# Scoring both differential heads of a pair in one run of 24 row-tiled products, in four banks, in a two-layer hybrid encoder

## The chip, the cores and the metric

The kernel runs on one core of one Trainium2 chip. The metric is the device time of one execution in microseconds (us). Engines are named as in the profile: PE is TensorE, DVE VectorE, ACT ScalarE, POOL GpSimd, SP SyncE, which issues most DMAs.

## The reference

Two layers are applied to x of 256 tokens by 2048 columns, in float32. Each layer projects the normed x to 7168 columns, feeds three groups of heads, and projects their joined outputs back. The group that the change touches is the differential attention: six heads, each with two halves of 64 columns in q and k, and one v of 128 columns.

```python
q = rmsnorm(d_q.reshape(b, s, DIFF_HEADS, 2, DIFF_HALF_DIM), diff_q_norm_g[l])
k = rmsnorm(d_k.reshape(b, s, DIFF_HEADS, 2, DIFF_HALF_DIM), diff_k_norm_g[l])
sc = jnp.einsum('bhcqd,bhckd->bhcqk', qi, kt) * scale + bias[None, :, None]
p = jax.nn.softmax(sc, axis=-1)
o = jnp.einsum('bhcqk,bhkd->bhcqd', p, vt)
return o[:, :, 0] - lam * o[:, :, 1]
...
y_d = rmsnorm(o_d, diff_head_norm_g[l]) * (1.0 - lam_init) * silu(d_g)
x = x + jnp.concatenate([y_a, y_d, y_m], axis=-1) @ w_out[l]
```

`bias` is minus the head's slope times the distance of the two positions. The other groups are a short gated convolution and a cross-attention of four heads into 256 memory tokens.

## The kernel before

**The stream of products.** Nearly all the time goes into products of float32 matrices. Each operand is split into hi and lo parts, and three products (hi·hi, hi·lo, lo·hi) stand for one (`products`, L301 to L307). Weights come in pieces of 256 rows by 512 columns: `load_w` (L286) has SP load a piece into `raw`, ACT round it to `hi` (L294) and DVE subtract to `lo` (L295). `raw` has four buffers, and so have `hi` and `lo` (`PARTS // CK`). `block` (L309) walks over the pieces of one block of 512 columns; a piece gives 12 products of 128x512 on PE. In this document these are the ordinary products, and "a piece" is 12 of them. The layer's input projection has 112 pieces, its output projection 27 more and some products of another form. Before the first layer, the memory tokens' keys and values are projected in the same way.

**Side work.** Everything else is written as generators that are stepped between the pieces. `later(g, n)` makes a generator due n pieces from now; `run_side` (L231) is called once per piece and steps those that are due; a `yield n` asks to be called n pieces later. Within the program, a scheduler that works from a time line may still shift instructions that are not pinned against each other; `pin` keeps an instruction in the written order of the pinned ones of its engine.

**The differential heads.** The projections of q and k are normed, turned to columns by DVE transposes of 32x32 blocks and a trip through DRAM (`turn_sheet`, `carry`), and split into `yT` (`qk_T`, L530). Then three generators `pair` per layer (L558) do two heads each. They begin at the fifth block of the projection (L1069 to L1074), nine pieces apart (`PAIR_EVERY`, L39); the two memory pairs follow in the same rhythm. A pair does this:

- For each head, wait for a free buffer `e` (there are two), then `diff_scores` (L599): 12 products of 64 rows (L606), two halves c of the head in the upper and lower 64 rows of PE's array, two blocks of tokens, three products each, into two banks of PSUM from the pool `ps_s` (tag s). Then DVE adds the bias out of PSUM (L611), takes the maximum (L613), ACT takes the exponentials with their sums (L617), and DVE forms the difference of the two halves (L620 to L624). Between the heads the generator lets two pieces pass.
- Turn both heads' weights (`sh`, L573) and carry them through DRAM (L498, L502).
- `weighted` (L514): four products of the weights with v into one bank of the pool `ps_t` (tag t) for each head, `po` (L519; the profile counts eight), and `diff_out` (L628), which norms and gates them; the result is turned and split into `yT` again.

**PSUM.** There are eight banks: four for the ordinary products, two in `ps_s`, two in `ps_t`. `ps_s` also serves the memory heads' scores (L661 to L663), `ps_t` also `po` of both kinds of heads.

Of the kernel before, what the change touches and what calls it, by code (L numbers as in the profile page):

```python
# [10 lines left out]
F32 = mybir.dt.float32  # L11
# [7 lines left out]
P = 128  # L19
D_MODEL = 2048  # L20
SEQ = 256
DEPTH = 2
NT = SEQ // P
# [4 lines left out]
CG = W_CONV // P  # L28
# [10 lines left out]
PAIR_EVERY = 9  # L39
# [9 lines left out]
def encoder(ctx: ExitStack, tc: tile.TileContext, x, mem, norm_g, w_in, conv_w, conv_b,  # L49
            dq_g, dk_g, lq1, lk1, lq2, lk2, head_g, mem_norm_g, w_mem_kv, mq_g, mk_g, w_out, out):  # L50
    nc = tc.nc
    x, mem, out = x[0], mem[0], out[0]

    def pool(name, bufs, space=None):
        kw = {"space": space} if space is not None else {}
        return ctx.enter_context(tc.tile_pool(name=name, bufs=bufs, **kw))
# [9 lines left out]
    ps_s = pool("ps_s", 2, PSUM)  # L66
    ps_t = pool("ps_t", 2, PSUM)
# [3 lines left out]
    def nm(s):  # L71
        uid[0] += 1
        return f"{s}_{uid[0]}"
# [136 lines left out]
    side, tasks = deque(), []  # L210
    due = {}
    chunk = [0]

    def later(g, n):
        due[id(g)] = chunk[0] + n
        return g
# [30 lines left out]
    made = set()  # L247
# [50 lines left out]
    def accumulators():  # L298
        return [ps_acc.tile([P, NB], F32, tag="acc", name=nm("acc")) for _ in range(NT)]
# [127 lines left out]
    def col(st, which, t):  # L427
        return st[:, which, t:t + 1]
# [64 lines left out]
    def carry(sheet, to):  # L493


        d = dram.tile([NA, B, NA, sheet.shape[-1]], F32, name=nm("d"))
        for a in range(NA):
            tc.keep_in_program_order(nc.sync.dma_start(d[:, :, a].rearrange("b c r -> c b r"), sheet[a * B:(a + 1) * B]))  # L498
        yield 2
        of = d.rearrange("b c a (n i) -> (b c) a n i", i=B)  # L500
        for a in range(NA):
            tc.keep_in_program_order(nc.sync.dma_start(to[:, :, a], of[:, a]))  # L502
# [25 lines left out]
    ROWS = (slice(0, HALF), slice(HALF, P))  # L528
# [25 lines left out]
    scored = set()  # L554

    held = {"e": 0, "sh": 0, "yn": 0}

    def pair(heads, begin, end, v):  # L558

        es = []  # L560
        for h in heads:
            while held["e"] == 2:
                yield 1
            held["e"] += 1
            es.append((yield from begin(h)))
            yield 2
        yield 4
        while held["sh"] == 2:
            yield 1
        held["sh"] += 1  # L570
        sh = tmp.tile([P, NA, 2, NT * NT, B], F32, tag="sh", name=nm("sh"))
        for i, e in enumerate(es):
            tc.keep_in_program_order(nc.vector.transpose(  # L573
                sh[:, :, i], e[0].rearrange("p t (k b c) -> p b (t k) c", k=NT, b=NA)))
            held["e"] -= 1
            yield 1
        yield 4
        flat = sh.rearrange("p b h n c -> p (b h n c)")
        yield from carry(sh.rearrange("p b h n c -> p b (h n c)"), flat.rearrange("p (n a i) -> p n a i", a=NA, i=B))
        eT = flat.rearrange("p (h t k q) -> p h t k q", h=2, t=NT, k=NT)  # L580
        while held["yn"] == 2:
            yield 1
        held["yn"] += 1
        yn = tmp.tile([P, NA, 2, NT, B], F32, tag="yn", name=nm("yn"))
        for i, h in enumerate(heads):
            end[0](h, yn[:, :, i], weighted(eT, i, v, h), *es[i][1:])
            yield 2
        held["sh"] -= 1
        yield 5
        tc.keep_in_program_order(nc.vector.transpose(yn, yn))  # L590
        yield 5
        flat = yn.rearrange("p b h t c -> p (b h t c)")
        yield from carry(yn.rearrange("p b h t c -> p b (h t c)"), flat.rearrange("p (n a i) -> p n a i", a=NA, i=B))
        for i, h in enumerate(heads):
            end[1](h, flat[:, i * SEQ:(i + 1) * SEQ])
            yield 1
        held["yn"] -= 1

    def diff_scores(l, h, yT):  # L599
        while not {("q", l, h), ("k", l, h)} <= made:  # L600
            yield 1
        s = [ps_s.tile([P, NT, SEQ], F32, tag="s", name=nm("s")) for _ in range(2)]
        for i in range(NT):
            for n, (a, b) in enumerate(((0, 0), (0, 1), (1, 0))):
                for c, rows in enumerate(ROWS):
                    pin(nc.tensor.matmul(s[c][:, i, :], yT[rows, a, h, i * P:(i + 1) * P], yT[rows, b, CG + h, :],  # L606
                                         start=n == 0, stop=n == 2))
        scored.add((l, h))
        e = tmp.tile([P, 2, NT, SEQ], F32, tag="e", name=nm("e"))
        for c in range(2):  # L610
            nc.vector.scalar_tensor_tensor(e[:, c], dist, -slopes[h], s[c], ALU.mult, ALU.add)  # L611
        mx = small.tile([P, 2, NT], F32, tag="mx", name=nm("mx"))
        nc.vector.tensor_reduce(mx, e, AX.X, ALU.max, negate=True)  # L613
        sm = small.tile([P, 2, NT], F32, tag="sm", name=nm("sm"))
        for c in range(2):
            for i in range(NT):
                nc.scalar.activation(e[:, c, i], e[:, c, i], AF.Exp, bias=mx[:, c, i:i + 1],  # L617
                                     accum_out=sm[:, c, i:i + 1])
        iv = small.tile([P, 2, NT], F32, tag="iv", name=nm("iv"), bufs=6)
        nc.vector.reciprocal(iv, sm)  # L620
        cf = small.tile([P, NT], F32, tag="cf", name=nm("cf"))
        nc.vector.scalar_tensor_tensor(cf, sm[:, 0], neglam[:, l:l + 1], iv[:, 1], ALU.mult, ALU.mult)
        for i in range(NT):
            nc.vector.scalar_tensor_tensor(e[:, 0, i], e[:, 1, i], cf[:, i:i + 1], e[:, 0, i], ALU.mult, ALU.add)  # L624
        return e[:, 0], iv
        yield

    def diff_out(h, yn, po, iv, st, a):  # L628
        ss = small.tile([P, NT], F32, tag="hss", name=nm("hss"))
# [180 lines left out]
    pin = tc.keep_in_program_order  # L810
# [48 lines left out]
    class Memory:  # L859
# [47 lines left out]
        def begin(self, half, part, w):  # L907

            if part == 0 and w == 0:
                self.acc[0, half] = accumulators()  # L910
            w_part = self.parts[0][w][:, half]
            for t in range(NT):
                pin(nc.tensor.matmul(self.acc[0, half][t], memT[:, part, 0, t * P:(t + 1) * P], w_part,  # L913
                                     start=part == 0 and w == 0, stop=False))
# [101 lines left out]
    s = 1  # L1016
    while s < DEPTH * KT:
        l, k = divmod(s, KT)
# [22 lines left out]
        s = group[-1] + 1  # L1041

    for l in range(DEPTH):
# [5 lines left out]
        yT = T_tile("yT")  # L1049
# [3 lines left out]
            return block(xT, w_in[l], cols, order, rows=x_row_tiles, **how)  # L1053

        def begin_pair(n, p):
            tasks.append(later(p, max(1, start + PAIR_EVERY * n - chunk[0])))


        order = range(6) if l == 0 else (3, 0, 1, 2, 4, 5)
# [1 line left out]
        for b in order:  # L1061
            if b in begun:
                acc = x_block([(C_D + b * NB, NB)], ALLK[-QT:], acc=begun[b])
            else:
                acc = x_block([(C_D + b * NB, NB)], ready=m.ready if l == 0 and b == order[0] else None)
            if b == 3:
                v = keep.tile([P, NT, W_DIFF], F32, tag="v", name=nm("v"))
                ga = keep.tile([P, NT, W_DIFF], F32, tag="ga", name=nm("ga"))
            if b == 4:  # L1069
                start = chunk[0]  # L1070
                for n in range(DH // 2):
                    begin_pair(n, pair((2 * n, 2 * n + 1), lambda h: diff_scores(l, h, yT),
                                       (lambda h, yn, po, iv: diff_out(h, yn, po, iv, st, ga),
                                        lambda h, y: split_T(yT, CG + h, y, hgain[:, l:l + 1], pin=True)), v))  # L1074
            if b < 3:
                tasks.append(later(qk_T(l, yT, normed(acc, HALF, st, sheets(("mqT", "mga", "e")[b])),
                                 (0, 0, 4) if b == 0 else (0, 4, 2) if b == 1 else None,
                                 (256, 0, 2) if b == 1 else (0, 2, 4) if b == 2 else None), 8))
            else:
                for t in range(NT):  # L1080
                    if b == 3:
                        nc.scalar.activation(v[:, t, 0:NB], acc[t], AF.Copy, scale=col(st, R, t))
                    elif b == 4:
                        nc.scalar.activation(v[:, t, NB:768], acc[t][:, 0:256], AF.Copy, scale=col(st, R, t))
                        silu2(ga[:, t, 0:256], acc[t][:, 256:512], st, t)
                    else:
                        silu2(ga[:, t, 256:768], acc[t], st, t)
# [12 lines left out]
        for t in range(NT):  # L1100
            a = tmp.tile([P, NB], F32, tag="nat", name=nm("a"), bufs=3)
# [97 lines left out]
        heads, convs = list(range(CG, KT)), list(range(CG))  # L1199
# [33 lines left out]
        x = [pl.tile([P, NB], F32, tag=tag, name=nm("x")) for pl, tag in ((ps_s, "s"), (ps_s, "s"), (ps_t, "t"), (ps_t, "t"))]  # L1233
# [71 lines left out]
```

## Time and profile before

| what | value |
|---|---|
| median of 3 runs | 923.93 us (923.77 to 924.42) |
| the profiled execution | 924.17 us, of which span 922.4 us |
| mean granted clock of PE | 0.999 |
| ordinary products of w_in and w_out, L305, memory part included | 3717 |
| scores of 64 rows, L606 | 144, first and last start at 210.1 and 685.1 us |
| DVE, share of the span | 77% |
| ACT, share of the span | 54% |

The span runs from the first to the last instruction. The profiled execution is the one that the trace shows; its time of 924.17 us stands beside the span of 922.4, and the 1.8 us between them lie around the instructions. A row of PE's timeline merges equal instructions that follow each other: the second number is then the time from the first one's start to the last one's end. Ordinary products overlap: each is shown as 0.39 us long, but the next one starts before it ends. What a thing costs on PE is therefore read from starts, not from durations.

### The profile page before, as it was taken

The page shows a single profiled execution, that of the slowest core. Times are in us where ns is not written, and L with a number is a line of the kernel's source. Part 1 is how long each engine was busy: PE and PEld are TensorE (multiplying, and loading weights), DVE is VectorE, ACT ScalarE, POOL GpSimd, SP SyncE. Part 2 cuts the span into 40 slices and gives each one's busy share as a digit, 9 for nine tenths or more (in the row PEclk, how much of TensorE's full clock was granted, in tenths as well). Part 3 has the DMA queues.
Part 4 walks back from the last instruction along what each step waited for, and adds up shares of the span by engine and source line. Part 5 has one row for each costly group of instructions (what it writes and reads, how often), then busy time and mean ns, then how long its engine had stood idle before and what let it go on. Part 6 is the DMA issues. An engine that isn't in the chain of part 4 may idle for free.

```text
span 922.4 us, 12464 instructions
## 1 busy us (share of the span) xinstructions
PE 917.2 (99%) x4209; PEld 755.4 (82%) x4209; DVE 713.4 (77%) x1281; ACT 494.0 (54%) x770; POOL 38.2 (4%) x68
## 2 busy tenths in 40 slices
PE   9999999999999999999999999999999999999998
PEld 6888888887788888888888888888788888888887
DVE  5579978757799797577789857778898788588686
ACT  5667644545545555545556544446545655446352
POOL 2434010000000000000000000000000000000000
PEclk9999999999999999999999999999999999999999
DMA  8989878885679999969777867986769898968842
GB/s 288 288 241 268 273 238 237 252 238 162 183 204 244 245 258 275 245 212 253 245 222 229 274 196 217 267 234 194 194 203 255 221 264 250 272 217 250 273 160 92
DMA packets 244560, 215.16 MB, mean 233 GB/s; under 512 B 131976, under 2 KB 171720, under 8 KB 244496
## 3 DMA queue, kind: packets, MB, share of 16 engines
q1 hardware_dynamic: 239520, 208.71, 78.7%
q0 software_dynamic: 3776, 4.59, 2.1%
q10 hardware_dynamic: 1200, 1.07, 0.3%
q8 instruction: 33, 0.54, 0.3%
q14 instruction: 31, 0.25, 0.1%
HBM read 193.30 MB, written 21.00 MB: 232 GB/s over the span
## 4 chain that ended last, share of the span: by engine, by line
PE 99%; ACT 0%; DVE 0%; issue 0%
PE acc L305 92%; PE x L351 1%; PE s L606 1%; PE po L519 1%; PE acc L351 1%; PE po L729 1%; PE acc L913 1%; PE pt L743 0%; PE s L663 0%; PE s L661 0%; PE s L662 0%; PE warm L128 0%; PE rest L305 0%; ACT hi L895 0%; DVE xs L1211 0%; ACT memT L261 0%
## 5 line engine op out<-in xcount | busy, mean ns | idle before, releaser
L305 PE MATMUL acc<-hi,xT 128*128 128x512 f32 x1792 | 561.6, 391 | 0.0
L294 ACT CAST hi<-raw 128x1024 fp32r<-128x1024 f32 x270 | 283.8, 1051 | 310.2 <-PE acc L305 244.8
L295 DVE TENSOR_TENSOR lo<-raw,hi 128x1024 fp32r<-128x1024 f32 x270 | 329.1, 1221 | 136.7 <-ACT hi L294 134.9
L305 PEld LDWEIGHTS acc<-hi,xT 128*128 128x128 f32 x1792 | 336.0, 188 | 71.2
L305 PE MATMUL acc<-lo,xT 128*128 128x512 f32 x896 | 349.1, 390 | 0.0
L305 PEld LDWEIGHTS acc<-lo,xT 128*128 128x128 f32 x896 | 168.3, 188 | 33.5
L305 PE MATMUL acc<-hi,yT 128*128 128x512 f32 (+1 forms) x432 | 134.2, 388 | 0.0
L305 PEld LDWEIGHTS acc<-hi,yT 128*128 128x128 f32 x432 | 81.0, 188 | 16.6
L305 PE MATMUL acc<-lo,yT 128*128 128x512 f32 x216 | 83.7, 388 | 0.0
L305 PE MATMUL acc<-hi,memT 128*128 128x512 f32 x248 | 78.1, 393 | 0.0
L305 PEld LDWEIGHTS acc<-hi,memT 128*128 128x128 f32 x248 | 46.1, 188 | 9.4
L896 DVE SCALAR_TENSOR_TENSOR lo<-raw,cva,hi 128x1024 fp32r<-128x1024 f32 (+1 forms) x34 | 41.0, 1219 | 15.2 <-ACT hi L895 15.1
L305 PE MATMUL acc<-lo,memT 128*128 128x512 f32 x124 | 48.0, 391 | 0.0
L305 PEld LDWEIGHTS acc<-lo,yT 128*128 128x128 f32 x216 | 40.6, 188 | 8.4
L895 ACT ACTIVATE hi<-raw,cva 128x1024 fp32r<-128x1024 f32 (+1 forms) x34 | 36.4, 1099 | 11.7 <-DMA raw<-in_w_mem_kv_dram 11.4
L305 PEld LDWEIGHTS acc<-lo,memT 128*128 128x128 f32 x124 | 23.3, 188 | 5.6 <-DVE lo L896 0.9
L377 ACT CAST hi<-wide 128x1024 fp32r<-128x1024 f32 x15 | 15.6, 1050 | 16.9 <-DVE wide L380 7.0
L617 ACT ACTIVATE e<-e,mx 128x256 f32<-128x256 f32 x48 | 23.8, 498 | 0.9 <-DVE mx L613 0.9
L760 POOL DMA_DIRECT2D xt<-in_x_dram x32 | 21.4, 676 | 19.7 <-DVE rsy L189 13.3
L377 DVE TENSOR_TENSOR lo<-wide,hi 128x1024 fp32r<-128x1024 f32 x15 | 18.1, 1221 | 3.9 <-ACT hi L377 3.7
L481 DVE STREAM_TRANSPOSE sh<-sh 128x1024 f32<-128x1024 f32 (+2 forms) x14 | 17.3, 1238 | 0.0
L264 ACT ACTIVATE xT<-xf,gx 128x256 fp32r<-128x256 f32 x32 | 14.3, 502 | 5.4 <-DVE xf L766 4.3
(202 smaller groups left out, 715.6 us busy)
## 6 DMA issues: line engine op xcount, KB each, us to landing
raw<-in_w_in_dram SPq DMA_DIRECT2D x192, 512.0 KB, 4.7
raw<-in_w_out_dram SPq DMA_DIRECT2D x54, 512.0 KB, 4.8
raw<-in_w_in_dram SPq DMA_DIRECT2D x64, 256.0 KB, 3.8
raw<-in_w_mem_kv_dram SPq DMA_DIRECT2D x30, 512.0 KB, 6.2
d<-sh SPq DMA_DIRECT2D x88, 128.0 KB, 4.1
sh<-d SPq DMA_DIRECT2D x72, 128.0 KB, 4.1
wide<-in_w_out_dram SPq DMA_DIRECT2D x10, 512.0 KB, 6.2
xs<-in_x_dram SPq DMA_DIRECT2D x4, 512.0 KB, 6.9
```

The source lines that it names most:

```text
L264: both = (nc.scalar.activation(hi, src, AF.Copy, scale=gain), nc.vector.scalar_tensor_tensor(lo, src, gain, hi.bitcast(F32), ALU.mult, ALU ...
L294: nc.scalar.copy(hi, raw)
L295: nc.vector.tensor_tensor(lo_, raw, hi.bitcast(F32), ALU.subtract)
L305: i = nc.tensor.matmul(acc, left, right, start=start, stop=stop)
L351: nc.tensor.matmul(acc, left[a], right[b], start=first and i == 0, stop=last and i == 2)
L377: return ((hi, pin(nc.scalar.copy(hi, src))), (lo, pin(nc.vector.tensor_tensor(lo, src, hi.bitcast(F32), ALU.subtract))))
L481: tc.keep_in_program_order(nc.vector.transpose(src, src))
L519: nc.tensor.matmul(po[:, t, :], eT[:, i, t, k, :], v[:, k, h * P:(h + 1) * P], start=k == 0, stop=k == NT - 1)
L617: nc.scalar.activation(e[:, c, i], e[:, c, i], AF.Exp, bias=mx[:, c, i:i + 1], accum_out=sm[:, c, i:i + 1])
L760: tc.keep_in_program_order(nc.gpsimd.dma_start(st[:, n], src[n * B:(n + 1) * B].rearrange("p (b r) -> b p r", b=NA)))
L895: both = (nc.scalar.activation(hi[:, j], raw[:, j], AF.Copy, scale=g), nc.vector.scalar_tensor_tensor(lo[:, j], raw[:, j], g, hi[:, j].bit ...
L896: nc.vector.scalar_tensor_tensor(lo[:, j], raw[:, j], g, hi[:, j].bitcast(F32), ALU.mult, ALU.subtract))
```

## The change

Both heads of a pair are scored before either is weighted. The pair first waits until no buffer `e` is in use, and takes both. `diff_scores` then issues 24 products without a break in the written order, for the second head first, into two banks of `ps_t`, then for the first head, into the two banks of `ps_s`. The rest of the former function is now `diff_weights`, run for one head after the other with two pieces between. The number that spaces the pairs grows by 2/3 for the third one, `round(9 * 2.667)` = 24 pieces behind the first instead of 18. The memory pairs begin where they did, 27 and 36 pieces behind the first.

```diff
@@ def pair(heads, begin, end, v):
-        for h in heads:
-            while held["e"] == 2:
-                yield 1
-            held["e"] += 1
-            es.append((yield from begin(h)))
+        while held["e"] > 0:
+            yield 1
+        held["e"] += len(heads)
+        scores = yield from begin[0](heads)
+        for h, s in zip(heads, scores):
+            es.append(begin[1](h, s))
             yield 2
         yield 4
@@
-    def diff_scores(l, h, yT):
-        while not {("q", l, h), ("k", l, h)} <= made:
+    def diff_scores(l, heads, yT):
+        while not {(x, l, h) for x in "qk" for h in heads} <= made:
             yield 1
-        s = [ps_s.tile([P, NT, SEQ], F32, tag="s", name=nm("s")) for _ in range(2)]
-        for i in range(NT):
-            for n, (a, b) in enumerate(((0, 0), (0, 1), (1, 0))):
-                for c, rows in enumerate(ROWS):
-                    pin(nc.tensor.matmul(s[c][:, i, :], yT[rows, a, h, i * P:(i + 1) * P], yT[rows, b, CG + h, :],
-                                         start=n == 0, stop=n == 2))
-        scored.add((l, h))
+        scores = [[pl.tile([P, NT, SEQ], F32, tag=tag, name=nm("s")) for _ in range(2)]
+                  for pl, tag in ((ps_s, "s"), (ps_t, "t"))]
+        for h, s in reversed(list(zip(heads, scores))):
+            for i in range(NT):
+                for n, (a, b) in enumerate(((0, 0), (0, 1), (1, 0))):
+                    for c, rows in enumerate(ROWS):
+                        pin(nc.tensor.matmul(s[c][:, i, :], yT[rows, a, h, i * P:(i + 1) * P], yT[rows, b, CG + h, :],
+                                             start=n == 0, stop=n == 2))
+            scored.add((l, h))
+        return scores
+
+    def diff_weights(l, h, s):
         e = tmp.tile([P, 2, NT, SEQ], F32, tag="e", name=nm("e"))
@@
-            tasks.append(later(p, max(1, start + PAIR_EVERY * n - chunk[0])))
+            tasks.append(later(p, max(1, start + round(PAIR_EVERY * n) - chunk[0])))
@@
-                    begin_pair(n, pair((2 * n, 2 * n + 1), lambda h: diff_scores(l, h, yT),
+                    begin_pair(n + n // 2 * 2 / 3, pair((2 * n, 2 * n + 1), (lambda heads: diff_scores(l, heads, yT),
+                                                                 lambda h, s: diff_weights(l, h, s)),
```

Line numbers behind the edit are five to six higher: scores of 64 rows are L609 after the change, the biased copies out of PSUM L617, the maxima L619.

What stands where on an engine is read from the order of its instructions. On PE, in the first layer's first pair, the second head's scores stood like this before (s_2022 and s_2023 are its two banks, acc the ordinary products):

```order
940 L305 MATMUL acc_1936<-hi_2054,xT_110 128x512
941 L305 MATMUL acc_1936<-lo_2055,xT_110 128x512
942 L305 MATMUL acc_1936<-hi_2054,xT_110 128x512
943 L606 MATMUL s_2022<-yT_1060 128x256
944 L305 MATMUL acc_1937<-hi_2054,xT_110 128x512
945 L305 MATMUL acc_1937<-lo_2055,xT_110 128x512
946 L606 MATMUL s_2023<-yT_1060 128x256
947 L606 MATMUL s_2022<-yT_1060 128x256
```

One score stood by itself, then came two ordinary products, then the other eleven scores. All six pairs had their second head in this form; the first head's 12 stood together. After the change, at the join of the two heads of the same pair (s_1958 and s_1959 are the second head's banks, s_1956 and s_1957 the first head's):

```order
912 L609 MATMUL s_1958<-yT_1060 128x256
913 L609 MATMUL s_1959<-yT_1060 128x256
914 L609 MATMUL s_1958<-yT_1060 128x256
915 L609 MATMUL s_1959<-yT_1060 128x256
916 L609 MATMUL s_1956<-yT_1060 128x256
917 L609 MATMUL s_1957<-yT_1060 128x256
918 L609 MATMUL s_1956<-yT_1060 128x256
919 L609 MATMUL s_1957<-yT_1060 128x256
```

The 24 scores, rows 904 to 927, have no ordinary product between them, in this pair and in the other five. The pairs' runs now stand ten pieces apart (first to second) and thirteen (second to third); the third pair's run has 36 ordinary products between it and the second pair's first `po`. In each layer one group of four `po` products is now parted 3 + 1, and two of the four groups of six memory scores 1 + 5, by ordinary products.

On DVE, at the third pair of the first layer, before the change (e_2597 is the second head's buffer, `lo` are weight pieces, L203 and L204 belong to the norm of an earlier head):

```order
352 L611 SCALAR_TENSOR_TENSOR e_2597<-dist,s_2583 128x512
353 L611 SCALAR_TENSOR_TENSOR e_2597<-dist,s_2584 128x512
354 L203 TENSOR_TENSOR rsa_2500<-rsa_2500,ht_2495 128x2
355 L295 TENSOR_TENSOR lo_2707<-raw_2704,hi_2706 128x1024
356 L613 TENSOR_REDUCE mx_2600<-e_2597 128x4
357 L204 SCALAR_TENSOR_TENSOR rsy_2499<-rsa_2500,rsy_2499 128x2
358 L295 TENSOR_TENSOR lo_2762<-raw_2759,hi_2761 128x1024
```

And after it (e_2635 and e_2707 are the two heads' buffers, L509 and L1109 steps of the memory heads' gate):

```order
358 L295 TENSOR_TENSOR lo_2780<-raw_2777,hi_2779 128x1024
359 L509 SCALAR_TENSOR_TENSOR a_2657<-th_2658,acc_2392 128x512
360 L617 SCALAR_TENSOR_TENSOR e_2635<-dist,s_2607 128x512
361 L617 SCALAR_TENSOR_TENSOR e_2707<-dist,s_2609 128x512
362 L617 SCALAR_TENSOR_TENSOR e_2635<-dist,s_2608 128x512
363 L617 SCALAR_TENSOR_TENSOR e_2707<-dist,s_2610 128x512
364 L1109 STREAM_TRANSPOSE sh_2149<-a_2657 128x16x32
365 L619 TENSOR_REDUCE mx_2638<-e_2635 128x4
366 L619 TENSOR_REDUCE mx_2710<-e_2707 128x4
367 L295 TENSOR_TENSOR lo_2798<-raw_2795,hi_2797 128x1024
```

Between two weight pieces DVE had two copies, or one maximum; it now has four copies, two maxima and two steps of the gate.

More of the change, by code (lines that the diff above doesn't have):

```diff
@@ L625, in diff_scores @@
         return e[:, 0], iv
-        yield
     def diff_out(h, yn, po, iv, st, a):
```

## The prediction

> **What bounds the kernel now.** Read first: the page's line of engines, VectorE's (DVE's) busy tenths in 40 slices, the chain that ended last; then, of the list of who waited for whom, the rows of TensorE (PE).
>
> ```profile
> PE 917.2 (99%) x4209; PEld 755.4 (82%) x4209; DVE 713.4 (77%) x1281; ACT 494.0 (54%) x770; POOL 38.2 (4%) x68
> ...
> DVE  5579978757799797577789857778898788588686
> ...
> PE 99%; ACT 0%; DVE 0%; issue 0%
> ```
>
> ```profile
> PE warm L128 <- DVE zeros L123: 1.2, 1, 1.2
> PE acc L913 <- ACT hi L895: 0.4, 1, 0.4
> ```
>
> PE is busy for 917.2 of the span's 922.4 us, the chain never leaves it, and it waits for another engine twice, both times in the first microseconds. So nothing around the scores makes PE wait today; what counts is how much of PE's own time the scores take, and whether the change creates a wait. The groups by line show the scores:
>
> ```profile
> L606 PE MATMUL s<-yT 64*128 64x256 f32 x144 | 14.0, 299 | 0.0
> ```
>
> These are 12 heads of 12 products, of 64 rows each. Three stretches of PE's timeline give their price. Columns: start, duration from the first start to the last end, operation, count.
>
> ```profile
> 209.78 0.39 PE L305 MATMUL acc<-hi,xT 128*128 128x512 f32 x1
> 210.10 0.97 PE L606 MATMUL s<-yT 64*128 64x256 f32 x12
> 211.00 0.50 PE L305 MATMUL acc<-hi,xT 128*128 128x512 f32 x1
> ...
> 213.67 0.62 PE L305 MATMUL acc<-hi,xT 128*128 128x512 f32 x2
> ...
> 215.71 0.62 PE L305 MATMUL acc<-hi,xT 128*128 128x512 f32 x2
> ```
>
> From 213.67 to 215.71 stand nine ordinary products: 2.04 / 9 = 0.2267 us each. A weight piece is 12 of them, 2.72 us. From 209.78 to 213.67 stand 12 ordinary products (those at 209.78 and 211.00, and ten behind them), 2.72 us, in a stretch of 3.89: **one run of 12 scores costs 1.17 us**. What the starts show is that most of it is the turn: the first score starts 0.32 after its predecessor, and the product behind the run holds the next one back as well.
>
> ```profile
> 217.07 0.39 PE L305 MATMUL acc<-hi,xT 128*128 128x512 f32 x1
> 217.39 0.38 PE L606 MATMUL s<-yT 64*128 64x256 f32 x1
> 217.70 0.50 PE L305 MATMUL acc<-hi,xT 128*128 128x512 f32 x1
> 218.03 0.40 PE L305 MATMUL acc<-lo,xT 128*128 128x512 f32 x1
> 218.36 0.97 PE L606 MATMUL s<-yT 64*128 64x256 f32 x11
> 219.26 0.73 PE L305 MATMUL acc<-hi,xT 128*128 128x512 f32 x2
> ...
> 221.44 0.61 PE L305 MATMUL acc<-hi,xT 128*128 128x512 f32 x2
> ```
>
> This is the pair's second head. It is torn: one score, two ordinary products, eleven scores. From 217.07 to 221.44 are 4.37 us with 12 ordinary products (three, and nine from 219.26 on): 4.37 − 2.72 = **1.65 us for a torn head**.
>
> **The change, part by part.** Removed: the trace has six pairs (three in each of two layers), so 6 runs of 12 and 6 torn heads, 18 runs in all. Put in: 6 runs of 24; the order shows all 24 in a row, with no ordinary product inside. Products are neither added nor removed.
>
> The price of 24: in the first fence 12 scores last 0.97 from first start to last end, and a lone score lasts 0.38 (second fence). The scores go in six couples (two row halves, two banks), so a further couple adds (0.97 − 0.38) / 5 = 0.118, and a second dozen 6 × 0.118 = 0.71. A run of 24 should cost 1.17 + 0.71 = 1.88 us. No run here shows the join between the two heads. Its extra cost lies between nothing, since it is the same kind of product on the same array, and a full turn, 1.17 − 0.71 = 0.46. I take nothing, because the five joins between couples inside a run show no more than 0.118.
>
> A first or second pair of a layer goes from 1.17 + 1.65 = 2.82 to 1.88: a gain of 0.94. The third pair's first head follows directly on the weighted sums (po) of the first pair, and the run is cheaper there:
>
> ```profile
> 265.28 0.40 PE L305 MATMUL acc<-hi,xT 128*128 128x512 f32 x1
> 265.52 1.06 PE L519 MATMUL po<-v,sh 128*128 128x128 f32 x8
> 266.50 0.98 PE L606 MATMUL s<-yT 64*128 64x256 f32 x12
> 267.41 0.50 PE L305 MATMUL acc<-hi,xT 128*128 128x512 f32 x1
> ...
> 270.04 0.61 PE L305 MATMUL acc<-hi,xT 128*128 128x512 f32 x2
> ```
>
> ```profile
> 258.93 0.40 PE L305 MATMUL acc<-hi,xT 128*128 128x512 f32 x1
> 259.16 1.06 PE L519 MATMUL po<-v,sh 128*128 128x128 f32 x8
> 259.98 0.48 PE L305 MATMUL acc<-hi,xT 128*128 128x512 f32 x1
> ...
> 261.20 0.62 PE L305 MATMUL acc<-hi,xT 128*128 128x512 f32 x2
> ```
>
> The first stretch is 4.76 us with 12 ordinary products, so po and scores cost 2.04; the second is 2.27 with six, so po alone costs 0.91. The run there costs 1.13, and the third pair gains 1.13 + 1.65 − 1.88 = 0.90. Per layer 0.94 + 0.94 + 0.90 = 2.78, **for two layers 5.56 us**.
>
> Against that stand new tears that the order shows. In each layer one po group goes 3 + 1 instead of 4, and two of the four memory-score groups go 1 + 5 instead of 6. What a tear of full-height products costs is in this stretch:
>
> ```profile
> 306.15 0.40 PE L305 MATMUL acc<-hi,xT 128*128 128x512 f32 x1
> 306.38 0.28 PE L661 MATMUL s<-parts 128*128 128x256 f32 x1
> ...
> 307.10 0.39 PE L305 MATMUL acc<-hi,xT 128*128 128x512 f32 x1
> ...
> 308.26 0.61 PE L305 MATMUL acc<-hi,xT 128*128 128x512 f32 x2
> ```
>
> Here 2.11 us hold six ordinary products (1.36) and six memory scores: 0.75, of which 0.72 (306.38 to 307.10) are their own, six at 0.12. The run as such costs 0.03. A po run costs 0.91, and eight at (1.06 − 0.28) / 7 = 0.11 are 0.89, so about 0.02. Four tears at 0.03 and two at 0.02 cost 0.16; at the price of a turn of 64-row products (0.46) the six would cost 2.8. I take 0.16: these products are full height, and the row is theirs.
>
> **Cover that the moves need.** DVE now has both heads' scores at once. Its rows, and ScalarE's (ACT):
>
> ```profile
> L295 DVE TENSOR_TENSOR lo<-raw,hi 128x1024 fp32r<-128x1024 f32 x270 | 329.1, 1221 | 136.7 <-ACT hi L294 134.9
> L611 DVE SCALAR_TENSOR_TENSOR e<-dist,s 128x512 f32<-128x512 f32 x24 | 15.3, 679 | 0.2
> L613 DVE TENSOR_REDUCE mx<-e 128x4 f32<-128x1024 f32 x12 | 14.6, 1216 | 0.2
> ```
>
> ```profile
> L294 ACT CAST hi<-raw 128x1024 fp32r<-128x1024 f32 x270 | 283.8, 1051 | 310.2 <-PE acc L305 244.8 <-DMA raw<-in_w_in_dram 26.2 <-issue 22.8
> L617 ACT ACTIVATE e<-e,mx 128x256 f32<-128x256 f32 x48 | 23.8, 498 | 0.9 <-DVE mx L613 0.9
> ```
>
> A weight piece's hi and lo have four buffers each, so a split starts when the piece four before it is done, three pieces (8.16 us) ahead of its use, and takes 1.05 + 1.22: it is ready 5.9 us early. Behind one lo, DVE now does four biased copies (2.7) and two maxima (2.4) ahead of the next lo: 6.4 us instead of a pace of 2.72, which eats 3.7 of 5.9, and PE's own run of 24 gives 1.9 back: 4.1 left. The next lo stands behind both heads' last steps and eight exponentials on ACT (8 × 0.50 = 4.0 us, partly beside the maxima), which takes 1.2 more: some 2.9 us are left. At the layer's third pair the order puts two gate steps of about 0.7 in the same burst: 7.8 us, less 2.72; with 1.9 from the scores and 0.9 from the po behind them, 3.7 are left. So I cost the bursts at nothing. If that cover were gone, every microsecond of lateness would be one of PE, since PE takes its products in order.
>
> The new wait is that for banks. Scores of one head of a pair now lie in the two banks that po uses. In the third pair they stand 36 ordinary products ahead of the second pair's po, which waits for the second of the four biased copies. Those copies stand behind the lo of a piece that is split when the product three pieces ahead begins: 2.3 for the split, 0.7 for a gate step, 1.4 for two copies, 4.4 us behind the scores, against 36 × 0.2267 = 8.2: 3.8 us to spare. Behind that po on PE stand all later products. On SP the transposed weights (sh) that po reads are read back three pieces earlier relative to the weight stream, while po itself stands less than one earlier, so that wait gets shorter. The third pair and the memory pairs end one piece later on PE at most, with seven pieces to the first product that reads their outputs: nothing.
>
> The kernel after is 924.17 (the profiled execution: span 922.4 and 1.8 around it) − 5.56 + 0.16 = 918.8. That execution lies 0.24 over the median of the runs shown (923.93), so the forecast for a median is **918.5 us**, 0.6% less.
>
> **A rule weighed.** The wait table above shows no PE wait for a bank. The Trainium skill, TensorEngine Tiling (Array Packing), section Restrictions and Gotchas, warns that row tiling raises the pressure on PSUM, because row tiles need banks of their own and software must keep users apart. By that rule, 24 scores in four banks would make po wait, which is the third rival; no run here shows such a wait.
>
> **The rivals.**
> 1. The join costs a turn: 6 × 0.46 = 2.8 less gain, 921.3. For it: the two halves write other banks and read other rows of yT. Against it: couples inside a run change their operands as well. The same page, section Key Properties, says that changing the mode drains the array but changing the tile does not; the 0.118 per couple agrees.
> 2. DVE's burst or ACT's exponentials reach PE: the cover of 2.9 to 3.7 us is misjudged by one or two, some 1 us of waiting at one or two of three pairs, 1 to 4 us in all: 920 to 922.5. For it: the twelfth slice of DVE's tenths, 254 to 277 us, where the third pair begins, is at 9 already. Against: no PE wait today.
> 3. The other side: po waits for a bank. The place is the second pair's po behind the third pair's scores, once a layer. It decides the sign when DVE is over 3.8 + 3.7 = 7.5 us later than worked out (0.2% of the time plus the gain is 7.3 us, 3.7 per layer). That happens if DVE reaches the copies only after both the rest of the gate work and the previous pair's chain. With 9 us of lateness PE stands 5.2 per layer, 918.5 + 10.4 = 928.9. Against: the order puts the copies right behind one lo and one gate step.
>
> **How the numbers follow.** Forecast 0.74, rival 1 0.08, rival 2 0.11, rival 3 0.07. The forecast's own range is 917.8 to 919.6: tears between nothing and three times my price, and couples at 0.10 to 0.13 in the second dozen. For 8 in 10 the range takes in most of rivals 1 and 2: 917.5 to 921.3. About 0.2% (1.85 us) is what a measurement of this kernel tells from no change. Faster by more than that (under 922.1): the forecast, rival 1 and most of rival 2, 0.89; within it 0.04; slower 0.07.
>
> **What would show it.** Right: six runs of 24 in PE's timeline, about 1.9 us each by the sum above, a busy time of PE near 912, and no new row in the waits of PE. Wrong: a wait of PE for DVE at the scores or po lines, a gap ahead of products with lo, or ordinary products inside the runs. A 24 that costs 2.3 would be rival 1.

## The result, and the profile after

| | before | after |
|---|---|---|
| median of 5 runs | 923.93 us (923.33 to 924.42) | 919.19 us (918.22 to 921.22) |
| ratio, 95% interval | | 0.9952 (0.9937 to 0.9966) |
| span of the profiled execution | 922.4 us | 917.4 us |
| PE busy | 917.2 us | 911.1 us |
| the 144 scores of 64 rows | 14.0 us | 10.1 us |

The kernel is 0.5% faster; 918.5 was forecast, and 919.19 lies inside the range. The list of PE's waits, in the kernel after (engine, what it made, for whom it waited: total, times, longest):

```profile
PE warm L128 <- DVE zeros L123: 1.2, 1, 1.2
PE pva L134 <- DMA va<-in_mem_norm_g_dram: 0.6, 1, 0.6
PE acc L305 <- DVE lo L295: 0.4, 1, 0.4
PE acc L305 <- DVE lo L901: 0.2, 1, 0.2
PE acc L918 <- ACT hi L900: 0.2, 1, 0.2
```

All but the third row lie in the first 15 us, where the memory tokens' weights come in. The third is new: once, in the middle of the first layer, PE stands before a product with `lo`. It isn't at a pair, as will be seen. PE's timeline at the first pair of the first layer:

```profile
209.65 0.39 PE L305 MATMUL acc<-hi,xT 128*128 128x512 f32 x1
209.97 1.69 PE L609 MATMUL s<-yT 64*128 64x256 f32 x24
211.59 0.50 PE L305 MATMUL acc<-hi,xT 128*128 128x512 f32 x1
...
213.99 0.39 PE L305 MATMUL acc<-lo,xT 128*128 128x512 f32 x1
214.21 0.62 PE L305 MATMUL acc<-hi,xT 128*128 128x512 f32 x2
```

From 209.65 to 214.21 are 4.56 us with 12 ordinary products (2.72): **a run of 24 costs 1.84 us**, where 1.88 was worked out. The other five, counted in the same way, cost 1.84 too. So a layer's first two pairs went from 2.82 to 1.84 each.

DVE's burst at that pair, and the four biased copies of the third pair:

```profile
212.30 2.47 DVE L617 SCALAR_TENSOR_TENSOR e<-dist,s 128x512 f32<-128x512 f32 x4
214.69 2.34 DVE L619 TENSOR_REDUCE mx<-e 128x4 f32<-128x1024 f32 x2
216.95 1.22 DVE L295 TENSOR_TENSOR lo<-raw,hi 128x1024 fp32r<-128x1024 f32 x1
...
281.33 2.47 DVE L617 SCALAR_TENSOR_TENSOR e<-dist,s 128x512 f32<-128x512 f32 x4
```

PE, where it uses that `lo`, and where the second pair's `po` follows the third pair's copies:

```profile
222.83 0.39 PE L305 MATMUL acc<-lo,xT 128*128 128x512 f32 x1
...
288.03 1.06 PE L519 MATMUL po<-v,sh 128*128 128x128 f32 x8
```

The `lo` behind the burst is done at 218.17 and used at 222.83: 4.7 us of cover were left (4.1 worked out). By the same reading the next one has 3.3 (2.9), and the one behind the third pair's burst 4.1 (3.7). The copies out of the banks end at 283.80, and `po` starts at 288.03: 4.2 to spare (3.8).

### The profile page after: what moved, and what is told of

It is laid out like the page before. It is cut to its first block, busy times and chain, and to the rows that moved or that the text cites. A ratio compares the mean times of both kernels' runs of the same rounds, so it can differ in the third digit from the quotient of the medians.

```text
span 917.4 us, 12473 instructions
## 1 busy us (share of the span) xinstructions
PE 911.1 (99%) x4209; PEld 753.6 (82%) x4209; DVE 712.2 (78%) x1281; ACT 492.8 (54%) x770; POOL 38.2 (4%) x68
## 4 chain that ended last, share of the span: by engine, by line
PE 98%; DMA 1%; SPq 0%; DVE 0%; ACT 0%; issue 0%; ACTq 0%
PE acc L305 91%; PE x L351 2%; PE po L519 1%; PE acc L351 1%; PE s L609 1%; DMA raw<-in_w_mem_kv_dram 1%; PE po L734 1%; PE pt L748 0%; SPq L818 0%; PE s L667 0%; PE s L666 0%; PE s L668 0%; SPq L881 0%; DVE lo L901 0%; DVE lo L295 0%; ACT hi L900 0%
## 5 line engine op out<-in xcount | busy, mean ns | idle before, releaser
L1166 ACT ACTIVATE sh<-acc,st 128x512 f32<-128x512 f32 (+1 forms) x16 | 8.9, 579 | 14.6 <-DMA d<-sh 11.7
```

## Where the missing half microsecond went

The span fell by 5.0 us, not by the 5.4 of the sum. The difference lies at the new wait. Nine rows of the timeline after lead to it (SPq is the queue that issues DMAs; in brackets the idle time ahead of a row and what ended it):

```profile
367.90 1.77 DVE L481 STREAM_TRANSPOSE sh<-sh 128x1536 f32<-128x1536 f32 x1
370.16 2.88 SPq L502 DMA_DIRECT2D sh<-d  x4
373.08 1.70 SPq L291 DMA_DIRECT2D raw<-in_w_in_dram  x2
374.82 2.50 SPq L498 DMA_DIRECT2D d<-sh  x4
375.32 1.05 ACT L294 CAST hi<-raw 128x1024 fp32r<-128x1024 f32 x1 [1.53 <-issue]
...
383.19 1.27 ACT L1166 ACTIVATE sh<-acc,st 128x512 f32<-128x512 f32 x2 [6.81 <-DMA d<-sh]
384.34 1.04 ACT L294 CAST hi<-raw 128x1024 fp32r<-128x1024 f32 x1
...
385.42 1.23 DVE L295 TENSOR_TENSOR lo<-raw,hi 128x1024 fp32r<-128x1024 f32 x1 [7.79 <-ACT hi L294]
...
386.70 0.50 PE L305 MATMUL acc<-lo,xT 128*128 128x512 f32 x1 [0.35 <-DVE lo L295]
```

This is the gated convolution's part of the layer. The sheet `sh` with the conv gates is transposed by DVE, written to DRAM (L498), and its buffer is then filled anew by ACT with scaled quarters of `ux` (L1166), which has to wait until the write-out has landed. ACT works in order: for 6.81 us it makes no `hi`, DVE for 7.79 no `lo`, and PE's cover runs out, and it stands idle for 0.35 us. Counted from starts the loss is larger: the product starts 0.74 us behind its predecessor instead of 0.23, the next ones are a little late too, and together that is about 0.6 us. The same place before:

```profile
371.53 1.77 DVE L481 STREAM_TRANSPOSE sh<-sh 128x1536 f32<-128x1536 f32 x1
...
375.18 2.59 SPq L498 DMA_DIRECT2D d<-sh  x4
...
379.77 0.62 ACT L708 CAST v<-sh 128x512 fp32r<-128x512 f32 x1
...
382.11 1.27 ACT L1160 ACTIVATE sh<-acc,st 128x512 f32<-128x512 f32 x2 [1.72 <-DMA d<-sh]
```

To set the two side by side, take one and the same ordinary product (the 361st with `lo` in the first layer):

```profile
360.38 0.39 PE L305 MATMUL acc<-lo,xT 128*128 128x512 f32 x1
```

```profile
357.47 0.40 PE L305 MATMUL acc<-lo,xT 128*128 128x512 f32 x1
```

The first is before's, the second after's. From there to the write-out's issue it is 14.80 us before and 17.35 after: 2.55 more. By these rows DVE isn't the reason, since its transposes end 1.88 us ahead of the issue before and 5.15 after; SP is, which after the change has the memory pair's read-back (370.16 to 373.04) and two weight loads to issue first. From issue to the end of ACT's wait it is 6.93 and 8.37: 1.44 more. And ACT comes to L1166 earlier: 20.0 us behind that product before, 18.9 after, because conversions of the memory pair (one L708 and the two L715 before, L713 and L720 after) stood ahead of it and now stand behind. 2.55 + 1.44 + 1.1 = 5.1, which is the growth from 1.72 to 6.81.

**Theory A** has two parts. Turns: a run of 64-row products among ordinary ones pays some 0.5 us once, however long it is (1.17 for a run of 12, less the 0.67 that a second dozen adds), and this is all that the change gains. The wait: the gain was cut by ACT's in-order wait at L1166, made longer by the third pair's and the memory pairs' new places. The **rivals**: the gain comes from the whole heads alone, or from the later third pair; and the last half microsecond is nothing but the uneven start of the kernel.

## Experiments

Each ran beside the kernel before on the same chip (its medians were 924.34 and 924.37 in the two groups). Since the start varies, a second measure is read from each trace: the stretch from the start of the two layers' 41st product with `lo` (near 126 us) to that of their 1091st (near 900). The rows of before and of the second experiment, which is one of the two that come out lowest:

```profile
125.92 0.39 PE L305 MATMUL acc<-lo,xT 128*128 128x512 f32 x1
...
904.22 0.39 PE L305 MATMUL acc<-lo,yT 128*128 128x512 f32 x1
```

```profile
126.22 0.39 PE L309 MATMUL acc<-lo,xT 128*128 128x512 f32 x1
...
899.01 0.39 PE L309 MATMUL acc<-lo,yT 128*128 128x512 f32 x1
```

| kernel | median, us | ratio to before, 95% | from | to | stretch | idle gaps of PE inside |
|---|---|---|---|---|---|---|
| before | 923.93 | | 125.92 | 904.22 | 778.30 | none |
| after | 919.19 | 0.9937 to 0.9966 | 125.79 | 899.23 | 773.44 | 0.35 |
| again | 919.17 | 0.9929 to 0.9956 | 126.38 | 900.78 | 774.40 | 0.76 |
| ux_later | 919.03 | 0.9929 to 0.9954 | 126.22 | 899.01 | 772.79 | none |
| bg_earlier | 919.98 | 0.9943 to 0.9968 | 126.25 | 899.04 | 772.79 | none |
| merge_unshifted | 919.30 | 0.9935 to 0.9960 | 125.87 | 899.63 | 773.76 | none |
| untorn_apart | 921.89 | 0.9962 to 0.9981 | 125.31 | 901.93 | 776.62 | 0.66 |
| shift_only | 924.55 | 0.9995 to 1.0013 | 125.25 | 903.68 | 778.43 | none |
| bg_later | 927.19 | 1.0016 to 1.0036 | 125.99 | 907.82 | 781.83 | 2.66, 2.06, 0.40 |

**again**: the changed kernel once more, unedited.

> The changed kernel itself, timed again beside the others. Theory A (the two quarters of ux on ScalarE wait for the write-out of the gates' sheet, one piece sooner in ScalarE's order than before the change, and the length of that DMA decides how late the weight pieces behind it are): the best runs near 918.2 us, the others up to 3 us above, median about 919.2. Theory B (the half microsecond is lost at the score runs, in banks or in VectorE's burst): the same times in every run, near 919, since nothing there depends on a DMA's length.

Measured 919.17 (918.30 to 920.73). The profiled execution took 920.73 and shows the wait in the other layer: ACT waited 6.3 us in the first layer, and PE showed no idle gap; in the second ACT waited 7.6 and PE stood for 0.76 at 795.8. So the wait belongs to the kernel, not to one layer, and whether it reaches PE differs from run to run. The spread of 2.4 us, which Theory A expected, doesn't part the theories: the kernel before, whose trace has no such gap, ran beside it from 923.32 to 925.28.

**ux_later**: the scaled quarters of `ux` come one piece later on ACT (`hi` copies and quarters are pinned in written order during that block; the lines that do this are left out below). The side products keep their places on PE.

```diff
-        scaled(both_rows(ux, 0, 4), acc, R2)
-        acc = x_block([(C_C, NB)])
+        held_x = acc
+        pin_hi[0] = True
+        acc = x_block([(C_C, NB)], between={10: lambda _: scaled(both_rows(ux, 0, 4), held_x, R2)})
+        pin_hi[0] = False
```

> The changed kernel, with the two quarters of ux pinned one weight piece later on ScalarE, where they stood before the change; TensorE's order stays. Theory A: the wait of 6.8 us on ScalarE falls to about 2, the gap of 0.4 us on TensorE ahead of a product with lo is gone, median 918.2 to 918.5 us and a spread under 0.6. Theory B: no change in median or spread.

Measured 919.03 (917.84 to 919.36). ACT's wait is 4.2 us in the first layer and 1.9 in the second. PE's list now has only rows of the start (all gaps lie before 15 us):

```profile
PE acc L309 <- DVE lo L905: 0.8, 2, 0.6
PE acc L309 <- ACT memT L261: 0.6, 1, 0.6
PE acc L922 <- ACT hi L904: 0.2, 1, 0.2
```

The stretch is 772.79, 5.51 under before's: the sum of the prediction but for its small terms. By the same measure the wait cost 0.65 us in after and 1.61 in again, though PE's idle gaps there are only 0.35 and 0.76. It can be placed: 12 ordinary products, from a layer's 399th product with `lo` to its 403rd, take 2.72 us in ux_later, in both layers. In after they take 3.37 in the first layer; in again 2.90 in the first and 4.12 in the second. The median and the spread missed what was expected (918.2 to 918.5, and under 0.6): the medians don't part the three kernels. The start to 126 us alone differs by up to 1.1 us between traces (125.25 to 126.38) in a part that no edit touches, which may be why. So the cost of the wait is shown in the profiled executions, not in the medians.

**bg_earlier**: the other end of the same wait; the write-out's transposes are due one piece earlier.

```diff
-        tasks.append(later(turn_bg(list(range(CG))), 9))
+        tasks.append(later(turn_bg(list(range(CG))), 8))
```

> The changed kernel, with the gates' sheet due to be turned and written out 8 pieces instead of 9 after the gate block, ScalarE's order as in the changed kernel. Theory A: the write-out ends about 2.7 us sooner, ScalarE waits about 4 us instead of 6.8, TensorE no longer waits: 918.2 to 918.6 us, small spread. Theory B: no change, 919.2.

In the trace, ACT waits 5.1 us in the first layer and 4.3 in the second, PE not at all behind 100 us, and the stretch is 772.79, the same as ux_later's. In the median, 919.98 (919.02 to 921.12), nothing is gained, where 918.2 to 918.6 was expected: by the time it is a miss. Its profiled execution is its fastest, and what lengthened the others stays open.

**merge_unshifted**: the 24 scores in one run, but the third pair left at its old place, 18 pieces behind the first.

```diff
-                    begin_pair(n + n // 2 * 2 / 3, pair((2 * n, 2 * n + 1), (lambda heads: diff_scores(l, heads, yT),
+                    begin_pair(n, pair((2 * n, 2 * n + 1), (lambda heads: diff_scores(l, heads, yT),
```

> The 24 scores in four banks, but the third pair begins 18 pieces behind the first as before the change. In the order the third run is torn 1 + 23 in both layers, the memory scores are whole, and ScalarE has ux where it was before the change. By the price of turns: 918.2 + 2 x (0.48 - 0.06) = 919.0 us if the torn run costs a turn and nothing else; Theory A adds that the spread is small. Rival: the 23 wait for banks that the first pair's weighted sums still hold, then a TensorE wait ahead of them and 920 or more.

Measured 919.30 with the smallest spread of all (919.09 to 919.67). ACT waits 1.7 us at the sheet in the first layer and 2.5 in the second, as before the change (1.7 and 2.7); no run of scores waits for a bank. The stretch is 0.97 above ux_later's: the third pair's run is torn there, 1 + 23, once a layer, and the group of memory scores is whole. So the merge alone brings 4.54 of the 5.51; the later third pair brings the last 0.97, and with it comes the wait at the sheet, which takes 0.65 or 1.6 back in the two traces. In the median the two kernels are alike (919.30 and 919.19): what the later third pair is worth on balance isn't shown.

**untorn_apart**: heads scored apart as before the change, but with the second head's scores in the banks of `ps_t`, which leaves each head in one whole run of 12. The third pair has its new place.

```diff
-        s = [ps_s.tile([P, NT, SEQ], F32, tag="s", name=nm("s")) for _ in range(2)]
+        pl, tag = ((ps_s, "s"), (ps_t, "t"))[h % 2]
+        s = [pl.tile([P, NT, SEQ], F32, tag=tag, name=nm("s")) for _ in range(2)]
```

> The two heads of a pair are scored apart again, but each in a whole run of 12, ordinary products between them; the third pair stands where the changed kernel has it, and so does all that follows. Theory A (each run of 64-row products among ordinary ones pays a turn, however long it is; so half of a pair's gain is the torn head that is gone, 1.65 - 1.17 = 0.48, and half the merge, 2 x 1.17 - 1.84 = 0.50): six pairs cost 6 x 0.50 = 3.0 us more than the changed kernel's, thus about 922.2, and from the second layer's and first layer's work behind 126 us on 772.8 + 3.0 = 775.8 us plus whatever wait the sheet's write-out brings. Rival (the gain is all the torn head; two whole runs of 12 cost as much as one of 24): 919.2, 772.8. Rival (all of it is the merge): as the kernel before but for its small terms, about 924.

Measured 921.89 (920.88 to 922.70); 922.2 was expected. PE's timeline at the first pair:

```profile
209.17 0.39 PE L305 MATMUL acc<-hi,xT 128*128 128x512 f32 x1
209.49 0.97 PE L607 MATMUL s<-yT 64*128 64x256 f32 x12
210.39 0.50 PE L305 MATMUL acc<-hi,xT 128*128 128x512 f32 x1
...
213.06 0.62 PE L305 MATMUL acc<-hi,xT 128*128 128x512 f32 x2
...
215.78 0.39 PE L305 MATMUL acc<-hi,xT 128*128 128x512 f32 x1
216.10 0.97 PE L607 MATMUL s<-yT 64*128 64x256 f32 x12
217.00 0.50 PE L305 MATMUL acc<-hi,xT 128*128 128x512 f32 x1
...
219.67 0.62 PE L305 MATMUL acc<-hi,xT 128*128 128x512 f32 x2
```

Each head costs 3.89 − 2.72 = 1.17 (209.17 to 213.06 and 215.78 to 219.67, with 12 ordinary products each). Two cost 2.34 where the run of 24 costs 1.84, and six pairs 3.0. ACT waits 7.1 us at the sheet in the first layer, and the 12 ordinary products there take 3.69 us instead of 2.72: 0.97 lost. Without this the stretch is 775.65, 2.9 over ux_later's. So the rivals fall: half of a pair's gain is the tear that is gone, half the merge.

**shift_only**: the kernel before, with the third pair at its new place and nothing else changed.

```diff
-            tasks.append(later(p, max(1, start + PAIR_EVERY * n - chunk[0])))
+            tasks.append(later(p, max(1, start + round(PAIR_EVERY * n) - chunk[0])))
@@
-                    begin_pair(n, pair((2 * n, 2 * n + 1), lambda h: diff_scores(l, h, yT),
+                    begin_pair(n + n // 2 * 2 / 3, pair((2 * n, 2 * n + 1), lambda h: diff_scores(l, h, yT),
```

> The kernel before with one thing changed: the third pair is begun at piece 24, not 18. Heads stay apart and torn. Theory A: no turn is saved at the first two pairs; at the third the runs of scores and of weighted sums mix otherwise (within 0.5 us a layer), and ScalarE's scaled quarters come one piece earlier as in the changed kernel and wait for the write-out, 0 to 1.6 us: 923.5 to 926. Rival (the later third pair itself brings part of the gain, since PE works with less disturbance there): under 922.5.

Measured 924.55 (923.59 to 926.90), ratio 1.0004: no difference, as Theory A has it. The later third pair is worth nothing by itself; it is worth something only in that it keeps the run of 24 whole. And it brings most of the wait without the merge: ACT stands at the sheet for 5.3 and 4.7 us in the two layers, against 1.7 and 2.7 before, and PE loses nothing by it yet.

**bg_later**: the suspected wait made larger. The write-out is due at 10 instead of 9, and the quarters of `ux` stay where the changed kernel has them (pinned, with `between={8: ...}`; these lines, like ux_later's, are left out below). On PE the memory heads' `po` groups come up to three pieces earlier by this, parted 1 + 5.

```diff
-        tasks.append(later(turn_bg(list(range(CG))), 9))
+        tasks.append(later(turn_bg(list(range(CG))), 10))
```

> The changed kernel with the suspected wait made larger: the gates' sheet is written out one weight piece later (due 10 instead of 9), while ScalarE's scaled quarters stay where the changed kernel has them. Theory A (ScalarE, which works in order, stands at the scaled quarters till the write-out has landed, and the splits behind it come late to PE): ScalarE waits about 6.8 + 2.7 = 9.5 us there, the cover of 6.8 is used up, and PE loses up to 2.7 us a layer more than in the changed kernel: 919.2 + 5 = about 924, with a gap in PE's stream before products with lo near 387 and 796 us. Rival (that wait is covered, and the changed kernel's last 0.5 us were lost at the start alone): 919.2, and no gap there.

Measured 927.19 (923.92 to 928.12). ACT's wait in the first layer, from its list of waits there, and PE's list for the whole execution:

```profile
ACT sh L1170 <- DMA d<-sh: 9.9, 1, 9.9
```

```profile
PE acc L309 <- ACT hi L296: 4.7, 2, 2.7
```

The gaps are there, 2.66 us up to 389.0 and 2.06 up to 802.0 (where ACT waited 9.3), of about the size expected, though ahead of products with `hi` and a few us later than expected. Over all traces, what PE stands follows what ACT waits: 1.7 to 6.3 us of waiting, no gap; 6.8, 0.35; 7.1 (untorn_apart), 0.66; 7.6, 0.76; 9.3, 2.06; 9.9, 2.66. What PE loses by starts follows it more closely: each of the four waits from 6.3 to 7.6 us is 6.2 us longer than what it cost among the 12 products there (6.34, 0.18; 6.81, 0.65; 7.13, 0.97; 7.56, 1.40). Past 6.2 us every further microsecond was one of PE in these. But the kernel lost 8 us, not 5. PE's timeline by windows says where the rest went; the column before the last two is PE's granted clock:

```profile
380.00:389.00 9.00, 6.34 (x29) 4.91 (x28) 0.16 (x2) 2.26 (x4) 0.00 (x0) 0.97 0.68 211
389.00:390.50 1.50, 1.50 (x4) 0.87 (x4) 1.50 (x3) 1.50 (x4) 0.00 (x0) 0.50 0.00 0
...
394.00:395.50 1.50, 1.50 (x5) 1.17 (x4) 1.48 (x2) 0.49 (x1) 0.00 (x0) 0.55 1.01 137
395.50:397.00 1.50, 1.50 (x11) 1.37 (x10) 0.71 (x2) 0.81 (x2) 0.00 (x0) 1.00 1.05 156
```

Behind the gap PE ran at a clock of 0.50 until about 395, with ordinary products 0.427 us apart instead of 0.227. A stretch of 208 ordinary products and 30 others, counted off alike, takes 56.91 us there (from 353.53 to 410.45) against 50.90 in ux_later (from 353.75 to 404.65): 6.0 more, of which the late product is 2.8 and the rest, 3.2, is what about 6.4 us at half the clock lose. The second layer's gap of 2.06 had no such tail; with the gap of 0.40 behind it, ahead of a memory `po`, that layer lost 3.0. The other executions agree: the five of the twelve with the lowest mean clock (0.995 and 0.996) took 927.75 to 928.12 us, and the one with a mean of 1.000 took 923.92, near the 924 that was expected. The Trainium skill, TensorE: Matmul & The Clock Gate, section Why this matters for your kernels, advises no idle gaps of PE over about 3 us, since the clock then falls back; here 2.66, a little less, was enough once, and 2.06 wasn't.

## Why the prediction was right, and where it was short

- **The bound.** Right: PE busy in 99% of the span, and what PE no longer did came off the time.
- **The price of 24.** 1.84 against 1.88; 0.04 too dear, 0.2 us in all. The second dozen adds 0.67 instead of 0.71. The join costs nothing (rival 1 falls).
- **The pairs.** Worked out 5.56 for two layers; with 1.84 the same sum is 5.8. untorn_apart bears out its two halves, 0.48 for the tear and 0.50 for the merge.
- **The new tears.** This term was too small: 0.16 was taken, and the 5.80 less the 5.51 by which the stretch fell leave 0.29, mostly because a torn `po` group isn't as cheap as its row of eight let it seem. PE after:

```profile
254.13 0.85 PE L305 MATMUL acc<-hi,xT 128*128 128x512 f32 x3
254.82 0.83 PE L519 MATMUL po<-v,sh 128*128 128x128 f32 x6
255.41 0.47 PE L305 MATMUL acc<-lo,xT 128*128 128x512 f32 x1
...
257.81 0.39 PE L519 MATMUL po<-v,sh 128*128 128x128 f32 x2
...
261.25 0.61 PE L305 MATMUL acc<-hi,xT 128*128 128x512 f32 x2
```

  From 254.13 to 261.25 are 7.12 us with 27 ordinary products (6.12): 1.00 for `po` in two parts, against 0.91 whole, so 0.09 a tear instead of 0.02. The memory scores' tears measured 0.02 where 0.03 was taken (a lone score costs 0.14 and five cost 0.63, six together 0.75). That the sum came out so near is in part luck, since the errors in the price of 24 and in the tears have opposite signs: the stretch without the wait fell by 5.51, and 5.40 was forecast.
- **The cover of DVE's bursts, and the banks.** Right, and each some 0.4 to 0.6 us better than worked out. Rivals 2 and 3 didn't come at their places.
- **The step that failed** is the one on the memory pairs: "The third pair and the memory pairs end one piece later on PE at most, with seven pieces to the first product that reads their outputs: nothing." It followed their outputs only to PE. Their read-back moved on SP to just ahead of another sheet's write-out, and their conversions on ACT moved behind an instruction that waits for that write-out. The price was 0.65 us in the profiled execution and 1.6 in again, and nothing in the traces of ux_later and bg_earlier, where ACT's wait was at most 4.2 and 5.1 us; their medians don't show it. It is of rival 2's kind (a split comes late to PE), but at a place that the prediction didn't look at.
- **From execution to median.** 0.24 us were taken off because the execution before lay over its median; the one after is its median. With the wait (0.65), less the terms' 0.11 and 0.13 of a quicker start, that makes 0.65 of the 0.7 between 918.5 and 919.19.

What the trace doesn't settle is the uneven start, and with it which run falls where between 917.8 and 921.2; no run tried it.

## What to carry over

Where few short products in another tile form stand among long ones, count the runs, not the products: each run paid about 0.5 us here (0.48 for a tear, 0.50 for a split into two runs), so work that is ready at about the same time is worth issuing as one block.
After moving side work, follow what it issues in every in-order queue, DMA issue included, to whatever stands next there, and look for an instruction that waits on a transfer ahead of the one that feeds the bound engine; moving that one instruction by one piece kept the wait from reaching PE in its trace, though the median didn't part the two kernels.
When the whole time varies by as much as the effect, measure a stretch of the trace between two products that all kernels have in common.

## What the runs showed of the hardware

- A run of 12 products of 64 rows cost 1.17 us, one of 24 cost 1.84, and one torn 1 + 11 cost 1.65: beside what each further couple adds, a run paid about 0.5 us whatever its length.
- An idle gap of PE of 2.66 us (bg_later) was followed by some 6 us at half the granted clock, which cost 3.2 us beside the late product's 2.8; one of 2.06 us wasn't. Each was seen once, in one trace.
- A wait of ACT, which makes the weight pieces in order, cost PE nothing up to 5.3 us, and 0.18, 0.65, 0.97 and 1.40 us at 6.34, 6.81, 7.13 and 7.56.
